# RWKV block kernel: the first pair's place in the projection stream, and the order of a block copy

## The chip, the core and the metric

The kernel runs on one core of a Trainium2 chip. The metric is the time of one execution on the device in microseconds (us), as the median of several runs: 2704.45 us for the kernel before (three runs, 2704.22 to 2705.92). A core has a matrix engine (TensorE, PE in the profile), a vector engine (VectorE, DVE), a scalar engine (ScalarE, ACT), GpSimd (POOL) and a sync engine (SP), each working off its own instructions in order, and 16 DMA engines that they share.

## What is computed

One residual block on 512 tokens of width 2048: a projection, two mixers side by side (RWKV-7 and sliding-window attention), merged by sigmoid gates, and a gated feed-forward layer with a short convolution. Cut to what matters here:

```python
h = rms_norm(x, norm1_g)
z = h @ w_in                       # r, k, v, three low-rank parts; q, k, v; two gates
o_rw = rwkv7_mix(token_shift(z_rw), ...)
o_att = swa_attention(q, k, v, ...)
x = x + (sigmoid(z_r) * (o_rw @ w_b1) + sigmoid(z_a) * (o_att @ w_b2)) @ w_out
x = x + conv_ffn(rms_norm(x, norm2_g), w_up, conv_w, conv_b, w_down)

def rwkv7_mix(...):                # per head, a state of 64 x 64, one token after the other
    def step(state, inp):
        r, k, v, w, ka, kb = inp   # ka = -kk, kb = kk * a, with kk the normalised key
        sa = state @ ka
        state = state * w + outer(sa, kb) + outer(v, k)
        return state, state @ r
    # then a group norm per head, a bonus term, and a gate g
```

## The kernel before

**Stages.** The program projects `z` tile by tile, does the attention while it goes on projecting, then the RWKV mixing, then the branch projection, the output projection, and the feed-forward layer. This case is about the RWKV stage, which in the profile lies between about 306 and 1101 us.

**The projection stream.** A column tile of `z` is 128 columns wide. `ztile` makes one of them by 48 matmuls (`project`, line 284 of the kernel): 16 blocks of the contraction, each taken three times, since weights and activations are split into a high half (`whi`, made by ScalarE at line 263) and a low half (`wlo`, made by VectorE at line 264). Weights come in groups of four blocks, 12 matmuls to a group, each by a DMA on SP's queue (line 260). Every stream matmul is put on the list `stream`, so that other work can be placed against its number. Of the 72 tiles 32 are gate tiles: `emit_gate` makes one, takes its tanh on ScalarE (line 383) and stores it to DRAM from ScalarE's queue. Gates depend on nothing in the RWKV stage and can be made at any time before the branch projection; the kernel uses them to fill TensorE.

**The pairs.** The 16 RWKV heads are done two at a time, as eight pairs `p` = 0 to 7. A pair has two parts:

- `early(p)` projects the pair's key, receptance and value (three tiles of the stream) and makes the decays, the norm of the keys and the bonus. The key norms are summed by small products (line 389), turned by TensorE (line 392), written to DRAM and read back broadcast to all partitions (lines 396 and 400, on SP's queue), and multiplied into `kk` by VectorE (line 675).
- `late(p)` scans. VectorE fills `BKK` and `BAR` (lines 691 to 694); `BAR`'s four writes have to wait for the last product of the pair before that reads `BAR`. TensorE makes the products of keys within 8 chunks of 64 tokens (line 711); VectorE masks them; then a triangular inverse is built up in five doubling levels of two groups of matmuls each (`mm3`, lines 760 and 763), between which ScalarE and VectorE combine results (lines 795 to 799 and 825 to 827). From the second level on, the block made so far is turned by TensorE (`turned`) and copied by `kept` (line 783: three copies on ScalarE, one on VectorE) into `BT`, which the level's second group reads. Last come the 8 chunks in sequence: `psG` (line 836), `psU` (841), the `UV` copies on ScalarE and VectorE (843, 844), `psS` (852), the state `SV` (858).

**What is hung in between.** The output of the pair before is finished inside the levels of the next: `normed` scales it to unit variance on VectorE (its sums begin at line 871, its last instruction, at line 880, scales `y`), right after the first level; `final` turns it, applies the gate and stores it after the fourth level. At the second level the state rows are copied into `UV` (line 805).

**The order of the work.** Loop over pairs: `late(p)`, one gate (not for `p` = 0), `early(p + 1)`, two more gates. So pairs 1 to 6 each bring 288 stream matmuls and pair 0 brings 240. The instructions of the pair would by themselves be issued as early as the planner thinks they can run. Instead the first instruction of each group is held: `entries` lists these (the transposes of the values, the ten groups of the levels, the transposes of `final`, the instructions of the chunks), `at` gives each a number of stream matmuls counted from the pair's `base`, and `behind(ins, stream[base + n - 1])` orders it behind that matmul, without a semaphore, since both are on TensorE. `LEVEL` holds the ten groups' numbers, `CHUNK` those of the chunks. Pair 0 has all of its numbers 4 lower (the first one 7). `pin` keeps marked instructions of an engine in program order.

**Behind the pairs.** The last pair's output is finished by `normed` and `final`, held at 317. The RWKV output is then read back from DRAM, split into halves (`rhi`, `rlo`) between the remaining gates, eight calls of `emit_gate` in all, and the attention output after them (`ahi`, `alo`).

Of the kernel before, what the change touches and what calls it, by code (L numbers as in the profile page):

```python
# [14 lines left out]
ALU = mybir.AluOpType  # L15
# [4 lines left out]
P = 128  # L20
# [3 lines left out]
C = 64  # L24
NCH = S // C
# [110 lines left out]
def block_kernel(ctx: ExitStack, tc: tile.TileContext, d: Dims, a: dict, out: bass.AP):  # L136
    nc = tc.nc
    act, dve, pool, pe, sync = nc.scalar, nc.vector, nc.gpsimd, nc.tensor, nc.sync
    NK, NP, NQ, NKV, NF = d.NK, d.NP, d.NQ, d.NKV, d.NF
# [84 lines left out]
    for f in range(NPRE):  # L224
        w, t = a["w_up"][f], {n: up_d[f, n] for n in ("s3", "s1", "P6", "P3")}
# [26 lines left out]
    def behind(ins, before):  # L252
        tc.add_manual_dep(ins.ins, before.ins.name,
                          mybir.DependencyInfo(mybir.DependencyClass.NoSync, mybir.DependencyReason.DATA))
# [41 lines left out]
    if True:  # L296
# [50 lines left out]
        with tc.tile_pool(name="x0_ps", bufs=1, space=PSUM) as ps0:  # L347
            ps = ps0.tile([P, S], F32, name="ps_r")
# [28 lines left out]
        def emit_gate():  # L377
            if not gates:
                return
            i = gates.pop(0)  # L380
            acc = ztile(d.c_zr + i * P)
            g = wp["gate"].tile([P, S], F32, name="gt", tag="gt")
            act.activation(g, acc, AF.Tanh, scale=0.5)
            act.dma_start(gate_d[i * P : (i + 1) * P], g)
# [19 lines left out]
        with ExitStack() as pt:  # L404
# [87 lines left out]
            for g in range(NHK):  # L492
# [7 lines left out]
                for n in range(NT):  # L500
# [37 lines left out]
                    ps = small()  # L538
# [13 lines left out]
        with ExitStack() as pr:  # L552
# [57 lines left out]
            for h, (lo, hi) in enumerate(HV):  # L610
                ol, oh = HV[1 - h]
# [72 lines left out]
            def late(p, st, norm, finish):  # L684
# [23 lines left out]
                for n0 in range(0, NCH, 2):  # L708
                    ps = bulk()
                    for j in range(2):  # L710
                        pe.matmul(ps[:, j * 2 * P : (j + 1) * 2 * P], BKK[:, n0 + j],  # L711
                                  BAR[:, n0 + j].rearrange("p h a c -> p (h a c)"), start=True, stop=True)
                    src = ps.rearrange("p (n q c) -> p n q c", n=2, q=4)
                    m2 = lambda nm: K[nm].unsqueeze(1).unsqueeze(1).to_broadcast([P, 2, 2, C])
                    dve.tensor_tensor(AB[:, n0 : n0 + 2], src[:, :, 0:4:3], m2("strict"), op=ALU.mult)
                    dve.tensor_tensor(W2[:, n0 : n0 + 2, 1:3], src[:, :, 1:3], m2("incl"), op=ALU.mult)
# [62 lines left out]
                def kept(ps):  # L779
                    dst = BT.rearrange("p e (q w) c -> p e q w c", w=2)  # L780
                    for w, (rl, rh) in enumerate(HV):
                        for h, (lo, hi) in enumerate(HV):
                            (dve.tensor_copy if w and h else act.copy)(dst[lo:hi, :, :, w, lo:hi], ps[rl:rh, :, :, lo:hi])

                for m in LEVELS[1:]:
                    last = m == LEVELS[-1]
# [11 lines left out]
                    dve.tensor_tensor(tt, tt, mask, op=ALU.mult)  # L798
                    done = dve.tensor_tensor(IW[:, :, 1], tt, IW[:, :, 0], op=ALU.subtract)
                    if m == LEVELS[1]:  # L800
                        norm(done)
                    if m == LEVELS[2]:
                        for h in range(2):
                            ol, oh = HV[1 - h]
                            behind(dve.tensor_copy(UV[ol:oh, :, h], SV[ol:oh, :, h]), done)
                    if xt is not None:
                        kept(xt)
                    ps = level_sum()
                    mm3(ps, BT, lambda n: IW[:, n], lambda n: IW[:, n, 0])
                    both = wk.tile([P, 2, NCH, HC], F32, name="tt", tag="dd")  # L810
# [56 lines left out]
            def normed(st, done):  # L867
                y = st[2]
                y3 = r3(y)
                st = wk.tile([P, 2, NCH], F32, name="st", tag="st")  # L870
                first = dve.reduce_sum(st[:, 0], y3, axis=AX.X)
                if done:
                    behind(first, done)
                dve.tensor_scalar(st[:, 0], st[:, 0], -1.0 / HD, None, op0=ALU.mult)
                dve.tensor_tensor(y3, y3, st[:, 0].unsqueeze(2).to_broadcast([P, NCH, C]), op=ALU.add)
                sq = wtile("gn")
                act.activation(sq, y, AF.Square)
                dve.reduce_sum(st[:, 1], r3(sq), axis=AX.X)
                rs = rsqrt_small(wk, st[:, 1], 1.0 / HD, GN_EPS, tag="rg")
                dve.tensor_tensor(y3, y3, rs.unsqueeze(2).to_broadcast([P, NCH, C]), op=ALU.mult)  # L880

            def final(p, st):
                ag, bon, y = st
# [17 lines left out]
                dve.tensor_tensor(yc, yc, ps, op=ALU.mult)  # L901
                pool.dma_start(o_rw_d[p], yc)

            entries = []
            ZT = 3 * NK
            LEVEL = [36, 51, 63, 76, 88, 102, 116, 131, 144, 158]
            CHUNK = [171 + 14 * n + 4 * (n > 2) + x for n in range(NCH) for x in (-5, 0, 4)][1:]
            st, lt, held = early(0), None, []
            for p in range(NP):
                entries.clear()  # L910
                base = len(stream)
                lt = late(p, st, lambda done: lt and normed(lt, done), lambda: lt and final(p - 1, lt))
                if p:
                    emit_gate()
                if p + 1 < NP:
                    st = early(p + 1)
                sums_along(up_jobs)()
                for _ in range(GATES_PER_PAIR * NK // 16 - 1):
                    emit_gate()
                at = [31, *LEVEL[:8], 137, *LEVEL[8:], *CHUNK] if p else [24, *(x - 4 for x in LEVEL + CHUNK)]  # L920
                held += [(ins, base + n - 1) for ins, n in zip(entries, at)]
            entries.clear()
            normed(lt, None)
            final(NP - 1, lt)
# [677 lines left out]
```

## Time and profile before

| what | value |
| --- | --- |
| time, median of three runs | 2704.45 us |
| the profiled execution's own time | 2706.29 us |
| its span, first to last instruction | 2704.5 us |
| mean granted TensorE clock | 0.998 |
| TensorE busy, whole span | 2667.4 us |
| VectorE busy | 1961.5 us |
| ScalarE busy | 1336.7 us |
| GpSimd busy | 232.7 us |

In the lists of waits a line reads: who waited, for what, how many us in total, how often, the longest. In the windows a line is a stretch in us from the span's start, its length, then each engine's busy time and (x) its instructions, the granted TensorE clock (1.00 is full speed), the mean busy share of the DMA engines, and GB/s. In the timeline a line is the start, the busy time, the engine, the line of the kernel, the operation, output and inputs, the shapes and the number of instructions merged into the line; in brackets stands how long the engine had been idle and what ended that. `PEld` is the loading of weights into TensorE, `SPq`, `POOLq` and `ACTq` are instructions of these engines' queues. Names are the program's: `acc` is a projection tile, `bulk` any of the pair's products.

### The profile page before, as it was taken

What the parts mean: (1) busy time and instruction counts of PE and PEld (TensorE: products, weight loads), DVE (VectorE), ACT (ScalarE), POOL (GpSimd) and SP (SyncE); (2) the same over time, 40 slices, a digit from 0 to 9 for tenths busy, and PEclk for the clock granted to TensorE, in tenths of its full rate; (3) what the DMA queues carried; (4) which work ended last, traced back from release to release, by engine and by line L of the source; (5) the groups of instructions that cost most, each with busy time, mean ns of one, the idle gap of its engine ahead of it and who ended that gap; (6) DMA issues with size and microseconds to landing.
All of it is one profiled execution on the core that took longest, in us unless ns stands there. A gap on an engine that the chain in (4) does not pass through costs nothing.

```text
span 2704.5 us, 45690 instructions
## 1 busy us (share of the span) xinstructions
PE 2667.4 (99%) x17410; PEld 1863.9 (69%) x17410; DVE 1961.5 (73%) x3380; ACT 1336.7 (49%) x2229; POOL 232.7 (9%) x323
## 2 busy tenths in 40 slices
PE   8999999999999999999999999999999999999999
PEld 4555566666666666555558999999999998555555
DVE  6787758777877774545678888888888888565665
ACT  6455435544544553322566655555555555444453
POOL 0001111111111101011000111111111110000000
PEclk9999999999999999999999999999999999999999
DMA  6566877889887778889785988988898888877775
GB/s 237 152 165 190 209 205 194 227 217 233 213 222 204 191 185 239 244 242 301 253 269 171 270 233 240 256 248 239 232 250 251 242 236 275 304 240 247 258 259 183
DMA packets 228331, 623.78 MB, mean 231 GB/s; under 512 B 24960, under 2 KB 45072, under 8 KB 227088
## 3 DMA queue, kind: packets, MB, share of 16 engines
q1 hardware_dynamic: 159552, 445.23, 49.4%
q0 software_dynamic: 37216, 136.33, 26.2%
q10 hardware_dynamic: 31344, 39.31, 4.2%
q8 instruction: 136, 2.23, 0.3%
q14 instruction: 83, 0.68, 0.1%
HBM read 571.16 MB, written 191.18 MB: 282 GB/s over the span
## 4 chain that ended last, share of the span: by engine, by line
PE 85%; DVE 7%; DMA 3%; issue 2%; ACT 2%; ACTq 0%; POOL 0%; SPq 0%; DVEq 0%; POOLq 0%
PE acc L284 26%; PE X L1227 18%; PE X L1090 10%; PE Y L1090 9%; PE Y L1227 9%; PE Z L1227 4%; DVE wlo L264 1%; PE psG L836 1%; PE psS L852 1%; PE bulk L711 1%; PE bulk L760 1%; PE mi L541 1%; DMA hraw<-h_dn 1%; DMA h_o<-gin 1%; PE psU L841 1%
## 5 line engine op out<-in xcount | busy, mean ns | idle before, releaser
L1081 DVE TENSOR_TENSOR wlo<-raw,whi 128x1024 bf16<-128x1024 f32 x210 | 256.5, 1224 | 192.0 <-ACT whi L1080 190.7
L284 PE MATMUL acc<-xhi,whi 128*128 128x512 f32 x1152 | 347.1, 425 | 10.4 <-ACT whi L263 10.4
L1080 ACT ACTIVATE whi<-raw 128x1024 fp32r<-128x1024 f32 x210 | 221.8, 1058 | 274.2 <-PE X L1090 124.5
L263 ACT ACTIVATE whi<-raw 128x512 fp32r<-128x512 f32 x352 | 218.6, 627 | 254.0 <-PE acc L284 149.0
L264 DVE TENSOR_TENSOR wlo<-raw,whi 128x512 bf16<-128x512 f32 x352 | 239.5, 687 | 136.9 <-ACT whi L263 104.8
L284 PE MATMUL acc<-xlo,whi 128*128 128x512 bf16 x1152 | 316.2, 383 | 0.7 <-DVE xlo L314 0.4
L284 PE MATMUL acc<-xlo,wlo 128*128 128x512 bf16 x1072 | 293.5, 380 | 0.0
L1227 PEld LDWEIGHTS <-wlo 128*128 128x128 bf16 x2464 | 237.6, 96 | 39.6 <-DVE wlo L1209 0.7
L284 PEld LDWEIGHTS acc<-xhi,whi 128*128 128x128 f32 x1152 | 211.7, 189 | 58.5 <-ACT whi L263 11.8
L1227 PEld LDWEIGHTS <-whi 128*128 128x128 bf16 x2464 | 228.0, 98 | 33.1 <-issue 0.2
L284 PEld LDWEIGHTS <-wlo 128*128 128x128 bf16 x1408 | 137.8, 100 | 150.0 <-issue 8.8
L284 PEld LDWEIGHTS <-whi 128*128 128x128 bf16 x1408 | 125.8, 101 | 151.6 <-issue 49.6
L1209 DVE TENSOR_TENSOR wlo<-raw,whi 128x1024 bf16<-128x1024 f32 x184 | 224.0, 1218 | 5.9 <-ACT whi L1207 5.8
L1207 ACT ACTIVATE whi<-a 128x1024 fp32r<-128x1024 f32 x124 | 130.7, 1054 | 191.6 <-DVE a L1202 188.9
L1207 ACT ACTIVATE whi<-raw 128x1024 fp32r<-128x1024 f32 x184 | 193.0, 1050 | 42.0 <-issue 21.8
L1209 DVE TENSOR_TENSOR wlo<-a,whi 128x1024 bf16<-128x1024 f32 x124 | 151.9, 1225 | 71.6 <-ACT whi L1207 71.6
L1227 PE MATMUL X<-b,whi 128*128 128x256 f32 (+1 forms) x1472 | 195.2, 280 | 0.2 <-DVE x L1105 0.2
L1227 PE MATMUL Y<-t,whi 128*128 128x256 f32 (+1 forms) x1408 | 186.2, 280 | 0.0
L1227 PE MATMUL X<-t,whi 128*128 128x256 bf16 (+1 forms) x1408 | 185.4, 280 | 0.0
L1280 DVE SCALAR_TENSOR_TENSOR c<-u,par,c 128x512 f32<-128x512 f32 x176 | 131.5, 748 | 41.8 <-ACT c L1271 41.7
L1090 PEld LDWEIGHTS <-hhi 128*128 128x128 bf16 x840 | 81.5, 97 | 104.1 <-issue 0.3
L1090 PEld LDWEIGHTS <-hlo 128*128 128x128 bf16 x840 | 72.8, 97 | 107.4 <-issue 27.9
(390 smaller groups left out, 4591.6 us busy)
## 6 DMA issues: line engine op xcount, KB each, us to landing
raw<-in_w_up_dram SPq DMA_DIRECT2D x170, 512.0 KB
raw<-in_w_z_dram SPq DMA_DIRECT2D x288, 256.0 KB
s_dn<-in_w_dn_dram POOLq DMA_DIRECT2D x88, 512.0 KB, 7.2
raw<-s_dn SPq DMA_DIRECT2D x88, 512.0 KB
raw<-in_w_up_dram POOLq DMA_DIRECT2D x80, 512.0 KB, 8.6
raw<-in_w_dn_dram SPq DMA_DIRECT2D x66, 512.0 KB
s_dn<-in_w_dn_dram SPq DMA_DIRECT2D x44, 512.0 KB
s_dn<-s_dn SPq DMA_DIRECT2D x44, 512.0 KB
```

What stands on the lines that cost most here:

```text
L263: act.activation(hi, raw, AF.Copy)
L264: dve.tensor_tensor(lo, raw, hi.bitcast(F32), op=ALU.subtract)
L284: stream.append(pe.matmul(acc, l, r, start=k0 + j == 0, stop=k0 + n == nk and j == len(ops) - 1))
L541: pe.matmul(ps, vhl[:, n - 1 + kb, g].rearrange("p e c -> p (e c)"), phl[i][:, kb].rearrange("p h c -> p (h c)"), start=kb == kbs[0] and i ...
L711: pe.matmul(ps[:, j * 2 * P : (j + 1) * 2 * P], BKK[:, n0 + j], BAR[:, n0 + j].rearrange("p h a c -> p (h a c)"), start=True, stop=True)
L1080: act.activation(whi, wr, AF.Copy)
L1081: dve.tensor_tensor(wlo, wr, whi.bitcast(F32), op=ALU.subtract)
L1090: pe.matmul(dst, l, r, start=fst and j == order[0], stop=lst and j == order[2], skip_group_check=True)
L1207: pin(act.activation(hi, t, AF.Copy))
L1209: return lambda: pin(dve.tensor_tensor(lo, t, hi.bitcast(F32), op=ALU.subtract))
L1227: pin(pe.matmul(ps, l, r, start=start and k == 0 and i == way[0], stop=k == KH - 1 and i == way[2], skip_group_check=True))
L1280: pin(dve.scalar_tensor_tensor(t, u[:, i, j + 1 : j + 1 + S], cw[:, j + 1, ci : ci + 1], t, op0=ALU.mult, op1=ALU.add))
```

## The change

Four things are changed.

1. `emit_gate()` behind `late(p)` is called for pair 0 as well. Pair 0 then has 288 stream matmuls, and since there are 32 gates in all, the last of the calls behind the pairs finds none left.
2. Pair 0's numbers are no longer 4 lower than the others' but 8 higher (`lag`), pair 1's are 4 higher, the other pairs' unchanged. Four of the ten level numbers are one higher for all pairs: 63, 76, 88 and 158 become 64, 77, 89 and 159.
3. The first product of pair 0 (line 711 of the kernel before) is held behind the twelfth stream matmul from the pair's base; no pair's first product was held before.
4. At the second level `kept` is called ahead of the copies of the state rows, and both these copies and the last scaling of `normed` are ordered behind `kept`'s copy on VectorE. At the other levels the call moves ahead only in the text. These are orders on one engine, without a semaphore.

```diff
@@ -708,8 +708,10 @@
                 for n0 in range(0, NCH, 2):
                     ps = bulk()
                     for j in range(2):
-                        pe.matmul(ps[:, j * 2 * P : (j + 1) * 2 * P], BKK[:, n0 + j],
-                                  BAR[:, n0 + j].rearrange("p h a c -> p (h a c)"), start=True, stop=True)
+                        ins = pe.matmul(ps[:, j * 2 * P : (j + 1) * 2 * P], BKK[:, n0 + j],
+                                        BAR[:, n0 + j].rearrange("p h a c -> p (h a c)"), start=True, stop=True)
+                        if n0 + j == 0:
+                            grams.append(ins)
                     src = ps.rearrange("p (n q c) -> p n q c", n=2, q=4)
                     m2 = lambda nm: K[nm].unsqueeze(1).unsqueeze(1).to_broadcast([P, 2, 2, C])
                     dve.tensor_tensor(AB[:, n0 : n0 + 2], src[:, :, 0:4:3], m2("strict"), op=ALU.mult)
@@ -780,7 +782,8 @@
                     dst = BT.rearrange("p e (q w) c -> p e q w c", w=2)
                     for w, (rl, rh) in enumerate(HV):
                         for h, (lo, hi) in enumerate(HV):
-                            (dve.tensor_copy if w and h else act.copy)(dst[lo:hi, :, :, w, lo:hi], ps[rl:rh, :, :, lo:hi])
+                            ins = (dve.tensor_copy if w and h else act.copy)(dst[lo:hi, :, :, w, lo:hi], ps[rl:rh, :, :, lo:hi])
+                    return ins
 
                 for m in LEVELS[1:]:
                     last = m == LEVELS[-1]
@@ -798,13 +801,14 @@
                     dve.tensor_tensor(tt, tt, mask, op=ALU.mult)
                     done = dve.tensor_tensor(IW[:, :, 1], tt, IW[:, :, 0], op=ALU.subtract)
                     if m == LEVELS[1]:
-                        norm(done)
+                        scaled_y = norm(done)
+                    part = kept(xt) if xt is not None else None
                     if m == LEVELS[2]:
+                        if scaled_y:
+                            behind(scaled_y, part)
                         for h in range(2):
                             ol, oh = HV[1 - h]
-                            behind(dve.tensor_copy(UV[ol:oh, :, h], SV[ol:oh, :, h]), done)
-                    if xt is not None:
-                        kept(xt)
+                            behind(dve.tensor_copy(UV[ol:oh, :, h], SV[ol:oh, :, h]), part)
                     ps = level_sum()
                     mm3(ps, BT, lambda n: IW[:, n], lambda n: IW[:, n, 0])
                     both = wk.tile([P, 2, NCH, HC], F32, name="tt", tag="dd")
@@ -877,7 +881,7 @@
                 act.activation(sq, y, AF.Square)
                 dve.reduce_sum(st[:, 1], r3(sq), axis=AX.X)
                 rs = rsqrt_small(wk, st[:, 1], 1.0 / HD, GN_EPS, tag="rg")
-                dve.tensor_tensor(y3, y3, rs.unsqueeze(2).to_broadcast([P, NCH, C]), op=ALU.mult)
+                return dve.tensor_tensor(y3, y3, rs.unsqueeze(2).to_broadcast([P, NCH, C]), op=ALU.mult)
 
             def final(p, st):
                 ag, bon, y = st
@@ -901,24 +905,25 @@
                 dve.tensor_tensor(yc, yc, ps, op=ALU.mult)
                 pool.dma_start(o_rw_d[p], yc)
 
-            entries = []
-            ZT = 3 * NK
-            LEVEL = [36, 51, 63, 76, 88, 102, 116, 131, 144, 158]
+            entries, grams = [], []
+            LEVEL = [36, 51, 64, 77, 89, 102, 116, 131, 144, 159]
             CHUNK = [171 + 14 * n + 4 * (n > 2) + x for n in range(NCH) for x in (-5, 0, 4)][1:]
             st, lt, held = early(0), None, []
             for p in range(NP):
                 entries.clear()
                 base = len(stream)
                 lt = late(p, st, lambda done: lt and normed(lt, done), lambda: lt and final(p - 1, lt))
-                if p:
-                    emit_gate()
+                emit_gate()
                 if p + 1 < NP:
                     st = early(p + 1)
                 sums_along(up_jobs)()
                 for _ in range(GATES_PER_PAIR * NK // 16 - 1):
                     emit_gate()
-                at = [31, *LEVEL[:8], 137, *LEVEL[8:], *CHUNK] if p else [24, *(x - 4 for x in LEVEL + CHUNK)]
-                held += [(ins, base + n - 1) for ins, n in zip(entries, at)]
+                at = [31, *LEVEL[:8], *([137] if p else []), *LEVEL[8:], *CHUNK]
+                lag = max(0, 8 - 4 * p)
+                held += [(ins, base + n + lag - 1) for ins, n in zip(entries, at)]
+                if p == 0:
+                    held.append((grams[0], base + 11))
             entries.clear()
             normed(lt, None)
             final(NP - 1, lt)
```

## The prediction

> **What bounds the kernel now.** I read the page's first part and its chain first, then the waits of TensorE over the RWKV stage, then windows pair by pair, and then the order of instructions around each wait that this gave.
>
> ```profile
> span 2704.5 us, 45690 instructions
> PE 2667.4 (99%) x17410; PEld 1863.9 (69%) x17410; DVE 1961.5 (73%) x3380; ACT 1336.7 (49%) x2229; POOL 232.7 (9%) x323
> PE 85%; DVE 7%; DMA 3%; issue 2%; ACT 2%; ACTq 0%; POOL 0%; SPq 0%; DVEq 0%; POOLq 0%
> ```
>
> TensorE is busy for 99% of the span and is 85% of the chain: whatever it idles, or does at a lower clock, is paid in full. The change adds and removes no matmul, so its worth is idle time of TensorE. In the RWKV stage that is little and well named (waited for: us in total, times, longest):
>
> ```profile
> PE psS L852 <- DVE UV L844: 4.9, 1, 4.9
> PE bulk L711 <- DVE BAR L693: 2.4, 1, 2.4
> PE bulk L760 <- DVE BT L783: 2.0, 6, 0.3
> PE bulk L760 <- DVE XIW L799: 1.5, 3, 0.6
> PE bulk L760 <- DVE XIW L827: 1.1, 2, 0.8
> PE bulk L711 <- DVE bon L681: 0.4, 1, 0.4
> ```
>
> Together 12.3 us. The windows say in which pair they fall: the first three rows run from the start of pair 0, 1 and 2 to the start of the next, then come the wait ahead of pair 0's first product, the wait of 4.9 us, and the stretch behind it.
>
> ```profile
> 306.27:404.94 98.67, 90.10 (x612) 58.98 (x612) 68.08 (x155) 42.28 (x92) 10.96 (x16) 0.97 0.78 202
> 404.94:493.34 88.40, 86.06 (x603) 56.42 (x603) 69.61 (x172) 42.14 (x93) 9.96 (x16) 1.00 0.81 206
> 493.34:586.20 92.86, 92.34 (x636) 61.11 (x635) 71.10 (x172) 45.08 (x98) 12.08 (x18) 1.00 0.86 224
> 306.27:308.63 2.36, 0.00 (x1) 0.04 (x1) 2.31 (x5) 0.59 (x2) 0.00 (x0) 1.00 1.03 335
> 374.90:380.08 5.18, 0.27 (x2) 0.00 (x1) 2.83 (x6) 0.63 (x1) 0.00 (x0) 0.85 1.06 303
> 380.08:385.15 5.07, 5.07 (x17) 3.05 (x17) 3.90 (x7) 0.00 (x0) 0.91 (x2) 0.50 0.48 120
> ```
>
> Idle time is length less TensorE's busy time: 8.57 us in pair 0, 2.34 in pair 1, 0.52 in pair 2, which stands for pairs 2 to 7. Pair 0 loses more than it idles: for 5.07 us behind the long wait the granted clock is 0.50, so half of that, 2.5 us, is lost to the clock. The prices sit in the first two pairs, which the change lays out anew.
>
> **The change part by part.** One matmul of the projection stream costs 0.223 us (120.72 / 541, the chain of waits behind the last pair); a gate's 48 cost 10.7.
>
> ```profile
> 1054.65 120.72 PE acc L284 x541
> ```
>
> Two conversions of VectorE at pair 0's start, and the tanh of a gate in the list of groups:
>
> ```profile
> 307.79 0.68 DVE L693 SCALAR_TENSOR_TENSOR BAR<-kk,Et 64x512 f32<-64x512 f32 x1
> 308.51 1.29 DVE L264 TENSOR_TENSOR wlo<-raw,whi 128x512 bf16<-128x512 f32 x2
> ```
> ```profile
> L383 ACT ACTIVATE gt<-acc 128x512 f32<-128x512 f32 x32 | 19.1, 597 | 65.9 <-PE acc L284 65.9
> ```
>
> *Gate ahead of pair 0, first product held back.* The gate's 48 matmuls now come where the key projection of early(1) came, and pair 0's first product waits for 12 of them: 12 x 0.223 = 2.7 us of work where TensorE stood idle for 2.36. L693, its input, ends at 308.5 and should be ready. The danger is VectorE, busy for 2.31 of those 2.36 us: the low halves of the gate's weights must be made before or beside it, one at 0.65 (half of the 1.29 row). With two of them pushed ahead of L693 the gain is 1.1; with none 2.36. I take 2.1, nearer the upper end, since the two conversions at 308.51 come behind L693 already and the stream ran on without a wait for them. The wait for bon (0.4) and pair 0's part of the XIW wait (0.6) come from the same crowded VectorE; the distances from first product to first groups hardly change (24 to 27 and 47 to 47 stream matmuls), so of this 1.0 I take 0.3 (0 to 1.0). With the gate go its four weight loads on SP, ahead of early(1)'s loads, the weight sum on SP and POOL that its loads count off, and a tanh and a store on ACT: the same instructions, one gate earlier, on queues with room (POOL 10.96 and ACT 42.28 busy of 98.67 in pair 0); I charge nothing, and at most the 0.6 of the tanh (L383) if ACT were full. Behind the held product wait only pair 0's own products and transposes.
>
> *Pair 0 with 288 stream matmuls in place of 240.* Its long wait is a chain:
>
> ```profile
> 362.27 0.27 PE L392 MATMUL bulk<-ident,rq 128*8 128x128 f32 x1 [0.15 <-DVE rq L207]
> 362.89 0.29 SPq L396 DMA_DIRECT2D rsd<-rsT  x1
> 368.99 1.11 SPq L400 DMA_DIRECT2D rsb<-rsd  x2
> 373.68 0.38 PE L841 MATMUL psU<-GY,BX 128*128 128x128 f32 x2
> 377.16 0.69 DVE L675 TENSOR_TENSOR kk<-kk,rsb 128x512 f32<-128x512 f32 x1 [5.04 <-DMA rsb<-rsd]
> 379.80 0.23 DVE L844 COPY UV<-psU 64x64 f32<-64x64 f32 x1
> ...
> 547.90 0.27 PE L392 MATMUL bulk<-ident,rq 128*8 128x128 f32 x1
> 552.15 1.12 SPq L400 DMA_DIRECT2D rsb<-rsd  x2
> 558.86 0.68 DVE L675 TENSOR_TENSOR kk<-kk,rsb 128x512 f32<-128x512 f32 x1
> 560.39 0.23 DVE L844 COPY UV<-psU 64x64 f32<-64x64 f32 x1 [0.26 <-ACT UV L843]
> ```
>
> The key norms of the next pair go through DRAM and back: from L392 to L675 14.9 us in pair 0, 11.0 in pair 2, where VectorE did not wait. In pair 0 VectorE stands at L675 for 5.04 us with the UV copy of a chunk behind it, whose product was ready at 373.7 + 0.4; TensorE runs dry at psS. Only pair 0 is packed so that early(1) must be through 86 stream matmuls (240 less 154) after its last level; the new layout gives 121 (288 less 167), and 130 are there in pairs 2 to 7, none of which has this wait. I take all of it: 4.9 + 2.5 = 7.4; if the trip is late again, none.
>
> [...]
>
> *Groups later in pair 1.* Pair 0's chunks ran 33 matmuls into pair 1 (273 against 240) and now end at 285 of 288. Pair 1 starts its levels with a free VectorE and 4 matmuls, 0.9 us, of extra room. Its 2.34 should fall towards the 0.52 of pair 2; I take 1.9 (1.0 to 2.34). The seam itself is not short: the first product of pair 1 came 3.5 us behind pair 0's last psG without a wait,
>
> ```profile
> 401.45 0.56 PE L836 MATMUL psG<-SV,BAR 128*128 128x64 f32 x4
> 404.94 3.69 PE L711 MATMUL bulk<-BAR,BKK 128*128 128x256 f32 x16
> ```
>
> and will have 13 stream matmuls (2.9 us), psU and psS between (0.38 for psU by its row, as much taken for psS), about 3.7 us.
>
> *Block copy first, six pairs.* At the second level of pair 2 VectorE goes:
>
> ```profile
> 517.49 0.42 DVE L799 TENSOR_TENSOR XIW<-tt,XIW 128x256 f16<-128x256 f32 x1
> 517.83 0.68 DVE L880 TENSOR_TENSOR yc<-yc,rg 128x512 f32<-128x512 f32 x1
> 518.53 0.86 DVE L805 COPY UV<-SV 64x512 f32<-64x512 f32 x2
> 519.41 0.43 DVE L783 COPY BT<-bulk 64x512 f16<-64x512 f16 x1
> 520.96 0.42 DVE L826 SCALAR_TENSOR_TENSOR tt<-bulk,XIW 128x256 f32<-128x256 f32 x1 [0.39 <-ACT XIW L825]
> ```
>
> With L783 right behind L799 the copy ends near 518.3 and not 519.84, 1.5 us earlier, and the group is held one matmul later. The 0.33 of each pair should go: 1.8 of 2.0 (1.0 to 2.0). Scaling and state copies, 1.54 us, then run in the room ahead of L826; what waits on them is far off (the output's transposes stand at 137, the chunks at 171). The other positions that move by one cost nothing: stream matmuls fill the place.
>
> *One gate less at the end.* The last group, at 317, has 163 stream matmuls behind it before the branch projection in place of 211.
>
> ```profile
> 1092.31 1.28 DVE L217 TENSOR_TENSOR rlo<-rin,rhi 128x512 bf16<-128x512 f32 x2
> 1102.34 4.91 DVE L217 TENSOR_TENSOR alo<-ain,ahi 128x512 bf16<-128x512 f32 x8 [3.05 <-ACT ahi L216]
> 1107.76 1.89 DVE L264 TENSOR_TENSOR wlo<-raw,whi 128x512 bf16<-128x512 f32 x3
> ```
>
> The last two halves of the RWKV output were made at 1092, a gate ahead of the attention halves at 1102; now they come beside these and can push the weight halves behind them by 1.28. TensorE did not wait there; I charge 0.3 (0 to 1.3).
>
> **Sum.** 2.1 + 0.3 + 7.4 + 1.9 + 1.8 - 0.3 = 13.2 us. The profiled execution took 2706.29 us, 1.84 above the median of 2704.45, so 2693.1 there and 2691.3 as a median. With all upper ends 15.1 (2689.4); with all lower ends but the long wait gone 9.2 (2695.3).
>
> **The rivals.** *The long wait comes back.* The trip's length may be a matter of DMA load and not of layout: over the long wait the DMA engines' share was 1.06, and L675 precedes the UV copy in pair 2 as well, which is only 12.5 us behind L392. A trip of 14.9 us would again stop VectorE. For it: the two legs took 6.1 and 8.2 us in pair 0. Against: no other pair waits. Price: the 7.4 stays, 13.2 - 7.4 = 5.8, so 2698.7. [...]
>
> *Given back later.* Behind the stage the transfers of the weight sums and of the stored factors have their own pace; if one of them is what really holds TensorE at the next stage, the gain is lost there. Against it: the chain from 1054 on is TensorE without a break for 120 us, and transfers are issued as loads are used, so they move along. Price: most of the 13, 2702 to 2705.
>
> *Slower: scaling and state copies push the next level.* They now stand ahead of L826 in six pairs. L826 may start until about 520.9 (now 520.96, less the 0.33, plus one matmul); with L783 ending at 518.3, 1.54 of copies and one weight half (0.65) it starts near 520.5. Should more of VectorE's queue move ahead of it, all beyond 0.4 us is paid six times. To end slower by 5.4 it takes (13.2 + 5.4) / 6 = 3.1 us per pair, five weight halves: 2710 or more. For it: in pair 1 the same chain made TensorE wait, 1.1 us at L827. Against: VectorE idles 0.39 just there.
>
> **How the numbers follow.** Forecast 0.70; the long wait back 0.14; given back 0.10; slower 0.06. Measurement of this kernel can tell about 0.2%, 5.4 us, from no change: faster means below 2699.0. The rival at 2698.7 lies on that edge; I count 0.09 of its 0.14 as faster. Faster 0.79, same 0.15, slower 0.06. The range of 2689 to 2699 holds the forecast's own 2689.4 to 2695.3 and that part of the first rival.
>
> **What would show it.** In the changed profile: no wait of psS for UV above 0.5 us and no clock of 0.50 within the stage; L711's first wait under 0.5; L760's six waits for BT gone; pair 1's idle time under 1 us; branch projection entered without a wait. A wait of DVE at L675 for rsb with psS behind it makes the first rival right; waits at L760 for XIW L827 in every pair the last; all waits gone and the same time, the second.

## The result and the profile after

The changed kernel takes 2716.19 us (median; 2703.11 to 2718.24) beside 2704.53 us (2697.18 to 2706.68) of the kernel before in the same measurement: a ratio of 1.0033, with a 95% interval of 1.0021 to 1.0046. It is slower by about 12 us, where 13 us less was forecast. Its profiled execution took 2716.8 us.

The first lines of its page:

```profile
span 2715.0 us, 45687 instructions
PE 2669.1 (98%) x17410; PEld 1867.8 (69%) x17410; DVE 1964.5 (72%) x3380; ACT 1337.8 (49%) x2229; POOL 233.9 (9%) x323
```

The matmuls are the same 17410 and TensorE's busy time grew by 1.7 us only, so the other 9 us are idle time. One window finds the place: from the first key-norm product (L392, ahead of pair 0) to the first transposes behind the output projection. In the kernel before:

```profile
286.84:1415.05 1128.21, 1113.65 (x6727) 693.10 (x6728) 772.47 (x1661) 499.76 (x994) 121.83 (x183) 1.00 0.82 226
```

and in the changed one:

```profile
286.52:1425.75 1139.23, 1115.55 (x6727) 697.00 (x6728) 774.41 (x1661) 500.41 (x994) 122.61 (x182) 0.99 0.81 224
```

The same 6727 matmuls take 11.0 us longer: idle time grows from 14.56 to 23.68 us, and busy time by 1.9 us, which I put down to the clock (its rows follow). The whole loss lies in this stretch. TensorE's waits there, in the changed kernel (psG, psU, UV and psS now stand at lines 840, 845, 848 and 856, the products of the levels at 762 and 765, the block copy at 785):

```profile
PE psS L856 <- DVE UV L848: 15.5, 5, 6.1
PE bulk L392 <- DVE rq L207: 3.0, 7, 0.5
PE acc L284 <- DVE rlo L217: 1.4, 2, 1.2
PE bulk L711 <- DVE bon L681: 1.0, 1, 1.0
PE bulk L762 <- DVE XIW L802: 0.3, 1, 0.3
PE bulk L762 <- DVE XIW L831: 0.3, 1, 0.3
```

Most of the forecast gains are there. The six waits for BT are gone, the waits for XIW fell from 2.6 to 0.6 us, and at pair 0's start 1.0 us for bon is left of 2.8. But the wait of psS for UV, which was to vanish, came five times, 15.5 us in place of 4.9. The windows of the first three pairs, and those where the clock was granted at half:

```profile
308.47:406.28 97.81, 89.52 (x614) 59.14 (x613) 66.50 (x153) 41.28 (x90) 10.99 (x16) 0.97 0.82 204
406.28:503.36 97.08, 93.80 (x636) 61.85 (x636) 71.92 (x174) 45.41 (x98) 11.88 (x17) 0.98 0.81 210
503.36:597.99 94.63, 92.47 (x637) 61.30 (x636) 71.41 (x173) 45.13 (x98) 11.76 (x17) 1.00 0.84 217
378.41:385.24 6.83, 3.30 (x10) 2.81 (x11) 5.40 (x11) 0.63 (x1) 0.81 (x1) 0.50 0.50 129
477.40:480.81 3.41, 3.18 (x10) 1.99 (x11) 2.83 (x7) 0.00 (x0) 0.00 (x0) 0.50 0.69 208
668.54:675.37 6.83, 6.17 (x19) 3.77 (x20) 5.01 (x10) 0.27 (x1) 1.42 (x3) 0.50 0.98 218
```

Before, pair 0 idled 8.57 us, pair 1 2.34 and pair 2 0.52. Now pair 0 idles 8.29 us, pair 1 3.28 and pair 2 2.16. Here is one of the new waits from beginning to end, in the part of pair 2 where early(3) runs (rows of the changed kernel's timeline):

```profile
553.50 0.50 SPq L242 DMA_DIRECT2D s_dn<-in_w_dn_dram  x1
...
557.82 0.27 PE L392 MATMUL bulk<-ident,rq 128*8 128x128 f32 x1 [0.43 <-DVE rq L207]
...
558.97 0.29 SPq L396 DMA_DIRECT2D rsd<-rsT  x1
...
559.32 0.50 SPq L242 DMA_DIRECT2D s_dn<-in_w_dn_dram  x1
...
563.80 1.12 SPq L400 DMA_DIRECT2D rsb<-rsd  x2
...
569.65 0.38 PE L845 MATMUL psU<-GY,BX 128*128 128x128 f32 x2
...
570.90 0.69 DVE L675 TENSOR_TENSOR kk<-kk,rsb 128x512 f32<-128x512 f32 x1 [2.03 <-DMA rsb<-rsd]
...
572.23 0.23 DVE L848 COPY UV<-psU 64x64 f32<-64x64 f32 x1
...
572.51 0.66 PE L856 MATMUL psS<-UV,W 128*128 128x64 f32 x4 [1.61 <-DVE UV L848]
```

The trip of the key norms through DRAM, L392 to L675, takes 13.1 us; in the kernel before it took 11.0 in the same pair. VectorE stands at L675 for 2.03 us, the copy of UV waits behind it in the same queue though its product is ready at 570.0, and TensorE runs dry. Two rows are new beside the norms' write at 558.97: weight sums at 553.50 (5.5 us ahead) and at 559.32 (0.35 us behind). The same queue in the kernel before:

```profile
542.03 0.50 SPq L242 DMA_DIRECT2D s_dn<-in_w_dn_dram  x1
...
549.16 0.29 SPq L396 DMA_DIRECT2D rsd<-rsT  x1
...
554.03 0.50 SPq L242 DMA_DIRECT2D P_u<-P_u  x1
...
555.21 0.51 SPq L242 DMA_DIRECT2D s_dn<-in_w_dn_dram  x1
```

There the sums stood 7.1 us ahead and 4.9 and 6.1 us behind the write: the second and third came only after the norms' read (552.15).

**What a weight sum is, and why it moved.** `sums_along` adds two quarters of a weight of the output projection (`s_o`) or of the feed-forward layer (`s_dn`), which are used in later stages: a copy within DRAM on SP's queue, then an adding DMA on GpSimd's. `load_w` calls it by a count of weight loads: after every third load, and ten more times 12 loads apart:

```python
extra = range(6 * NK + 5, 6 * NK + 5 + 12 * (HELD // 3), 12)
...
wp["n"] += 1
...
elif wp["n"] % wp["step"] == 0 or wp["n"] in extra:
    sums_along()()
```

A pair of 288 stream matmuls has 24 loads, a whole number of both cycles, so every pair gets its sums at the same places. Pair 0 had 20 loads and now has 24: **the moved gate's four loads shift the sums of all later pairs by four loads.** The extra ones came at a pair's 1st and 13th load, and now come at its 9th and 21st. The trip of the key norms falls at about the 22nd load. With only ten of them, an extra sum stands ahead of the norms' write in pairs 0 to 4 alone (5.5 to 7.9 us ahead), and these are the five pairs that wait; in pairs 5 and 6, without one, the trips took 11.4 and 11.0 us.

**The theories.** A: the sums' new places lengthen the norms' trip; VectorE stands at L675 with the UV copy behind it. A2 (formed on the way): what hurts is an extra sum about 5.5 us ahead of the norms' write together with a regular one right behind it. B: the new layout itself makes the trip or the chunk late, wherever the sums are. C: the room that a mended wait gives back is lost to another wait. D: the seven new waits at L392 come of the last level's group being held at 159 in place of 158.

### The profile page after: what moved, and what is told of

Its sections match the earlier page's. It is cut to its first block, busy times and chain, and to the rows that moved or that the text cites. A ratio compares the mean times of both kernels' runs of the same rounds, so it can differ in the third digit from the quotient of the medians.

```text
span 2715.0 us, 45687 instructions
## 1 busy us (share of the span) xinstructions
PE 2669.1 (98%) x17410; PEld 1867.8 (69%) x17410; DVE 1964.5 (72%) x3380; ACT 1337.8 (49%) x2229; POOL 233.9 (9%) x323
## 4 chain that ended last, share of the span: by engine, by line
PE 89%; DVE 4%; DMA 3%; issue 2%; ACT 1%; POOL 0%; SPq 0%; DVEq 0%; ACTq 0%; POOLq 0%
PE acc L284 29%; PE X L1232 18%; PE X L1095 11%; PE Y L1095 9%; PE Y L1232 9%; PE Z L1232 4%; PE psS L856 1%; DMA rsb<-rsd 1%; PE psG L840 1%; PE bulk L762 1%; PE bulk L711 1%; PE mi L541 1%; DMA xi<-in_x_dram 1%; DVE wlo L264 1%; DMA rsd<-rsT 1%
## 5 line engine op out<-in xcount | busy, mean ns | idle before, releaser
L284 PE MATMUL acc<-xhi,whi 128*128 128x512 f32 x1152 | 348.1, 426 | 10.4 <-ACT whi L263 10.1
L284 PE MATMUL acc<-xlo,whi 128*128 128x512 bf16 x1152 | 318.1, 383 | 0.7 <-DVE xlo L314 0.4
L284 PE MATMUL acc<-xlo,wlo 128*128 128x512 bf16 x1072 | 293.6, 381 | 0.0
L284 PEld LDWEIGHTS acc<-xhi,whi 128*128 128x128 f32 x1152 | 213.3, 190 | 60.5 <-ACT whi L263 11.6
L284 PEld LDWEIGHTS <-wlo 128*128 128x128 bf16 x1408 | 138.1, 99 | 152.2 <-issue 11.2
L284 PEld LDWEIGHTS <-whi 128*128 128x128 bf16 x1408 | 126.3, 101 | 152.3 <-issue 50.5
```

The costliest lines, as they stand in the source:

```text
L284: stream.append(pe.matmul(acc, l, r, start=k0 + j == 0, stop=k0 + n == nk and j == len(ops) - 1))
```

## The experiments

**Sums shifted back in the changed kernel.** The count is raised by 2 ahead of pair 0's gate, which puts the extra sums at a pair's 7th and 19th load and the regular ones where pairs 1 to 7 of the kernel before had them.

```diff
+                if p == 0:
+                    wp["n"] += 2
                 emit_gate()
```

> The changed kernel, with the count of weight loads by which the weight sums are issued (every third load) advanced by 2 ahead of pair 0's gate, so that in every pair the sums come at the loads at which they came in pairs 1 to 7 of the kernel before. Theory A (the gate's four loads shifted the sums by one load against the key norms' trip through DRAM, and a sum's 512 KB now travels with it): the sum on SP is issued 4 to 5 us behind the norms' write and not 0.3 to 2.4, the write's leg (to the issue of the read back) is 2.4 to 3.5 us in most pairs, psS waits for UV less than 3 us in all (15.5 in the changed kernel), the clock is 1.00 through the stage, 2692 to 2699 us. Theory B (the new positions themselves, groups later and block copy first, bring the wait; the sums have no part): 10 to 16 us of psS waiting for UV, 2710 to 2718 us.

Measured: 2700.96 us (2695.22 to 2705.48), ratio 0.9988 (0.9979 to 0.9997). Nothing of the layout was undone, and 15 us were gone. The median lies 2 us above A's range; in the profiled execution (2695.22, the fastest of its twelve) three shorter waits of psS remain:

```profile
PE psS L856 <- DVE UV L848: 3.6, 3, 1.6
```

Two of them, in pairs 3 and 4, follow trips of 13.1 and 12.2 us that had a single sum near, 7.4 us ahead of the write. A trip can then be late with one sum too.

**Sums shifted in the kernel before.** The count is lowered by 2 at the end of pair 0. The regular sum then comes 0.3 us behind the norms' write in pairs 2 to 5 and 0.4 in pair 6, as in the changed kernel, but the extra ones do not come ahead of it.

```diff
                 held += [(ins, base + n - 1) for ins, n in zip(entries, at)]
+                if p == 0:
+                    wp["n"] -= 2
```

> The kernel before, with nothing changed but the count of weight loads set back by 2 at the end of pair 0, so that in pairs 1 to 7 the sums come at the loads at which they come in the changed kernel. Theory A: the wait of psS for UV appears in two to five of the trips that follow pair 0's, 6 to 14 us in all beside the 4.9 of pair 0, with half clock behind the longer ones: 2711 to 2722 us. Theory B: as the kernel before, 4.9 us of such waits and 2702 to 2707 us.

Measured: 2704.43 us (2701.3 to 2709.96), ratio 0.9998 (0.999 to 1.0007). A missed: the regular sum right behind the write harms nothing by itself; the trips of pairs 2 to 6 stayed at 11.0 us, and only pair 0 waits, for 1.7 us. That led to A2.

```profile
PE psS L852 <- DVE UV L844: 1.7, 1, 1.7
```

**An intermediate shift of the changed kernel.** As in the first experiment, by 1 in place of 2. In pairs 1 to 4 the extra sum then comes 7.4 us ahead of the norms' write and the regular one 5.5 us ahead, and none right behind it. In pair 2:

```profile
541.40 0.55 SPq L242 DMA_DIRECT2D s_dn<-in_w_dn_dram  x1
...
543.34 0.50 SPq L242 DMA_DIRECT2D s_dn<-in_w_dn_dram  x1
...
548.81 0.29 SPq L396 DMA_DIRECT2D rsd<-rsT  x1
```

> The changed kernel, with the count advanced by 1 ahead of pair 0's gate: the third of the three possible phases, every sum one load (about 3.6 us) earlier against the trip than in the changed kernel, so that SP's half of a sum comes 3 to 4 us ahead of the norms' write and GpSimd's half lands on the trip. Theory A: the trip still has company, write leg 4 to 6 us, psS waits 3 to 12 us in all, 2698 to 2712 us. Theory B: as the changed kernel, 2710 to 2718 us with 10 to 16 us of waits.

Measured: 2710.76 us (2703.61 to 2714.81), ratio 1.0016 (1.0007 to 1.0026), between the two kernels and within A's range:

```profile
PE psS L856 <- DVE UV L848: 10.4, 6, 3.0
```

Six waits, 10.4 us in the profiled execution (2704.72, one of the faster ones). The five largest are those of pair 0 and of pairs 1 to 4, whose trips took 12.1 to 14.4 us with both sums ahead of the write; with the regular sum alone at 5.5 us ahead, in pairs 5 and 6, they took 11.0 and 11.7. So the two places that A2 names are too narrow: two sums near the trip cost a good part also when both stand ahead of the write.

**VectorE's scaling of the keys held behind a UV copy.** The sums stay where the change put them. L675 alone is ordered behind the UV copy of the fourth chunk of the pair that is scanned, so VectorE no longer stands ahead of the copy that TensorE needs.

```diff
+            uvs = []
...
-                pin(dve.tensor_tensor(kk, kk, rb, op=ALU.mult))
+                ins = pin(dve.tensor_tensor(kk, kk, rb, op=ALU.mult))
+                if uvs:
+                    behind(ins, uvs[3])
...
+                uvs.clear()
...
-                    dve.tensor_copy(UV[C:P, n, 1], ps[C:P, 1])
+                    uvs.append(dve.tensor_copy(UV[C:P, n, 1], ps[C:P, 1]))
```

> The changed kernel, with VectorE's product of the keys with their norms (line 675) ordered behind the UV copy of the fourth chunk, about 17 us behind the turning of the norms, in place of ahead of the third chunk's copy. The sums stay where the change put them. Theory A and theory B both say that the trip is as long as before (11 to 16 us) but stops nothing: psS waits under 2 us in all, clock 1.00, 2692 to 2699 us. A rival C (the transfers on the DMA engines are what is late, and whatever needs them next waits instead: the weight halves or the next pair's first products): the waits turn up at L284 or L711, and the time stays above 2704 us.

Measured: 2696.64 us (2693.63 to 2699.12), ratio 0.9967 (0.9955 to 0.9979). One instruction moved, and 19.6 us of the changed kernel's time are gone. The waits above 0.3 us in the stage are then

```profile
PE bulk L392 <- DVE rq L207: 3.0, 7, 0.5
PE acc L284 <- DVE rlo L217: 1.5, 2, 1.3
```

No wait for UV, no half clock in the stage, and nothing has turned up in its place: C fell. The same part of pair 2, by its timeline (L677 is the scaling, L853 the UV copy):

```profile
546.03 0.27 PE L392 MATMUL bulk<-ident,rq 128*8 128x128 f32 x1 [0.42 <-DVE rq L207]
...
553.90 1.12 SPq L400 DMA_DIRECT2D rsb<-rsd  x2
...
558.53 0.23 DVE L853 COPY UV<-psU 64x64 f32<-64x64 f32 x1 [0.26 <-ACT UV L852]
...
564.29 0.23 DVE L853 COPY UV<-psU 64x64 f32<-64x64 f32 x1
...
564.54 0.69 DVE L677 TENSOR_TENSOR kk<-kk,rsb 128x512 f32<-128x512 f32 x1
```

The scaling now comes 18.5 us behind L392 and waits for nothing, and early(3) is none the worse for it: there was room all along.

**The ten extra sums moved alone.** The layout stays changed and the regular sums stay where they are; the extra ones come three loads later.

```diff
-    extra = range(6 * NK + 5, 6 * NK + 5 + 12 * (HELD // 3), 12)
+    extra = range(6 * NK + 8, 6 * NK + 8 + 12 * (HELD // 3), 12)
```

> The changed kernel, with the list of extra weight sums (ten loads, twelve apart, at which a sum is issued beside every third load) moved by three loads, so that in each pair an extra sum falls on loads 0 and 12 and no more on 9 and 21; the sums at every third load stay where the change put them. Theory A2 (the trip of the key norms is late where an extra and a regular sum stand within some 6 us of each other around it; one sum alone is harmless): the extra sum at 5.5 us ahead of the norms' write is gone in trips 2 to 5, the trip falls to 11.0 us there without a wait, psS waits 0 to 4 us in all (pair 0 may keep some), 2695 to 2702 us. Theory B2 (the layout makes the trip late by itself, the regular sum at 0.3 us being enough there): 10 to 16 us of psS waits, 2710 to 2718 us.

Measured: 2699.49 us (2695.07 to 2702.51), ratio 0.9981 (0.9973 to 0.999), within A2's range. Trips of pairs 1 to 6 are back at 10.5 to 11.8 us, and of psS's waits pair 0's 2.5 us and 0.4 are left:

```profile
PE psS L856 <- DVE UV L848: 2.9, 2, 2.5
```

**The changed kernel's sum places in the old layout.** The kernel before, with its count lowered by 8 at the end of pair 0, which brings the regular sums of pairs 1 to 6 and the extra ones of pairs 1 to 4 where the changed kernel has them by their trips; one extra sum comes ahead of pair 5's trip in place of pair 0's. No other part of the change is made.

```diff
+                if p == 0:
+                    wp["n"] -= 8
```

> The kernel before, with nothing changed but the count of loads set back by 8 at the end of pair 0, so that in pairs 1 to 5 both the regular and the extra sums come at the very loads of a pair at which they come in the changed kernel (extras on loads 9 and 21). Theory A2: an extra sum appears 5 to 6 us ahead of the norms' write beside the regular one at 0.3, trips of 12 to 15 us, psS waits in most of the trips 2 to 5, 5 to 12 us in all beside pair 0's, 2709 to 2720 us. Theory B2: trips of 11.0 us in pairs 1 to 7, as with the regular sums shifted alone, 2702 to 2707 us.

Measured: 2717.1 us (2708.62 to 2720.6), ratio 1.0045 (1.0032 to 1.0058). The old layout with the new sum places is as slow as the changed kernel. Its largest wait in the stage (those for BT are as before, 2.0 us), and one of the late trips:

```profile
PE psS L852 <- DVE UV L844: 12.0, 5, 4.6
```

```profile
543.11 0.50 SPq L242 DMA_DIRECT2D s_dn<-in_w_dn_dram  x1
...
547.04 0.27 PE L392 MATMUL bulk<-ident,rq 128*8 128x128 f32 x1
...
548.30 0.29 SPq L396 DMA_DIRECT2D rsd<-rsT  x1
...
548.64 0.50 SPq L242 DMA_DIRECT2D s_dn<-in_w_dn_dram  x1
...
554.66 1.12 SPq L400 DMA_DIRECT2D rsb<-rsd  x2
...
561.32 0.69 DVE L675 TENSOR_TENSOR kk<-kk,rsb 128x512 f32<-128x512 f32 x1 [3.23 <-DMA rsb<-rsd]
```

Sums stand 5.2 us ahead of the norms' write and 0.3 behind it, and the trip takes 14.3 us where it took 11.0: the changed kernel's picture, without its layout. B falls. Pair 5 of this run has both sums too and no wait (11.0 us), so the two sums make a late trip likely and not certain.

**The hold in the kernel before.** The same edit at L675.

> The kernel before with only VectorE's line 675 ordered behind the fourth chunk's UV copy, as in the run that held it in the changed kernel. Both theories: pair 0's wait of 4.9 us and its half clock go, nothing else moves: 7.4 us by the sum of the prediction, so 2696 to 2699 us. Then the changed kernel held in the same way (2696.6) is worth 0 to 3 us more or less than the old layout, and what was forecast for the rest of the change (6 us) was given back inside it. If it is at 2702 or more, the hold costs something that the first run of it hid.

Measured: 2700.51 us (2698.4 to 2706.43), ratio 0.999 (0.9981 to 0.9998), a little above what was expected: at the median 3 to 4 us are won by it, not the 7.4 that the prediction read from the profiled execution with its long wait. The times of the kernel before spread over 9 us (2697.18 to 2706.68), so its wait need not be 4.9 us in each execution. In the profiled one two sums stood near pair 0's trip, an extra one 2.3 us ahead of the norms' write and a regular one 1.0 us behind it; they belong to pair 1's first two loads, which are issued that early. In the two runs of the old layout with a shifted count only one stands there, 2.3 us ahead, and pair 0's wait is 1.7 and 1.2 us. So the old long wait too looks like a matter of sums; no run moved that sum alone.

**Last level's group back at 158, with the hold, in the changed kernel.**

```diff
-            LEVEL = [36, 51, 64, 77, 89, 102, 116, 131, 144, 159]
+            LEVEL = [36, 51, 64, 77, 89, 102, 116, 131, 144, 158]
```

> The changed kernel with line 675 held, and the last level's second group back at 158 from 159. The changed kernel has a new wait of 0.38 to 0.50 us at line 392 in seven pairs, behind the chain of 13 small instructions of VectorE that starts when the last level's products are through. Theory D (that one matmul of delay at the last level is what makes the chain late): the waits at L392 fall below 0.25 each, 1.5 us in all are won, 2694 to 2696 us against 2696.6. Theory E (the chain is late because the block copy or other work of VectorE moved): the waits stay at 0.4 and the time at 2696 to 2697.

Measured: 2695.67 us (2692.64 to 2695.91), ratio 0.9967 (0.9954 to 0.998). The waits at L392 fall from seven to two:

```profile
PE bulk L392 <- DVE rq L207: 0.7, 2, 0.5
```

D is right for the waits. The time's 1 us against the hold alone is within the spread of either.

**The block copy behind the state copies again, with the hold, in the changed kernel.** This undoes the fourth part of the change alone.

```diff
-                    part = kept(xt) if xt is not None else None
                     if m == LEVELS[2]:
-                        if scaled_y:
-                            behind(scaled_y, part)
                         for h in range(2):
                             ol, oh = HV[1 - h]
-                            behind(dve.tensor_copy(UV[ol:oh, :, h], SV[ol:oh, :, h]), part)
+                            behind(dve.tensor_copy(UV[ol:oh, :, h], SV[ol:oh, :, h]), done)
+                    if xt is not None:
+                        kept(xt)
```

> The changed kernel with the hold (kk's scaling behind the fourth UV copy) and with the fourth part of the change alone undone: at the second level the state copies and the scaling of y go ahead of the turned block's copy again. The prediction priced this part at 1.8 us (1.0 to 2.0), six waits of TensorE for BT of about 0.33 each. If that price is right: six waits for BT at the third level's product come back, about 2 us together, and the time is 2698 to 2699 beside 2696.6 with the hold alone. Rival: TensorE's first product of the second group is then late for another input as well (XIW or the next level's group), because the copies only changed places: fewer or no BT waits and a time within 0.7 us of 2696.6.

Measured: 2702.52 us (2699.17 to 2706.98), ratio 0.9995 (0.9986 to 1.0004), more than was expected. The waits for BT are back, with one in pair 0 as well:

```profile
PE bulk L766 <- DVE BT L789: 2.6, 7, 0.4
...
PE bulk L715 <- DVE bon L685: 1.1, 1, 1.1
...
PE bulk L715 <- DVE BAR L697: 0.6, 1, 0.6
```

The rival (waits that only change places) fell. Between the two profiled executions (2700.76 with this edit, 2696.75 with the hold alone) lie 4.0 us: 2.6 are the waits for BT, and 1.7 are waits at pair 0's start that this edit does not touch and that come and go between executions (0.98 us for bon in the changed kernel, none with the hold). The medians lie 5.9 us apart; what is beyond these waits is not accounted for.

**All three mends together** in the changed kernel: the hold, 158, and the extra sums three loads later.

```diff
-    extra = range(6 * NK + 5, 6 * NK + 5 + 12 * (HELD // 3), 12)
+    extra = range(6 * NK + 8, 6 * NK + 8 + 12 * (HELD // 3), 12)
...
-            LEVEL = [36, 51, 64, 77, 89, 102, 116, 131, 144, 159]
+            LEVEL = [36, 51, 64, 77, 89, 102, 116, 131, 144, 158]
```

> The changed kernel with all three mends: the hold, the last level's number back from 159 to 158, and the ten extra weight sums moved by three loads. Theory: with the hold, VectorE's stand at the scaling of kk costs TensorE nothing, so moving the sums as well wins nothing more: 2695 to 2697, as with the hold and 158 alone (2695.7). Rival: the late sums also cost elsewhere in the stage, or their move keeps the norms' trip short enough that early work behind kk is ahead in the next pair: 2692 to 2694. No wait of psS for UV in either case; waits at L392 under 0.5 in at most two pairs.

Measured: 2694.3 us (2693.08 to 2697.51), ratio 0.9971 (0.996 to 0.9983). It falls between the two ranges, and its interval overlaps those of the hold alone and of the hold with 158: once VectorE no longer stands ahead of the copy, where the sums lie cannot be told from the time. These three are the fastest versions measured, each about 0.3% below the kernel before.

## Why the prediction was wrong

**The failed step** is the largest term of the sum, 7.4 us for pair 0's long wait: "Only pair 0 is packed so that early(1) must be through 86 stream matmuls" and, with 121 in the new layout, "I take all of it". Two things were wrong in it.

- *The measure of room.* The stream matmuls left behind the last level say when early(p + 1) must end. The wait hangs on another distance, from L392 to the next UV copy that stands behind L675 on VectorE, and that the new layout did not change. The rows give it: a trip less the wait that it caused is 10.0 us in pair 0 before (14.9 less 4.9) and 9.9 to 10.0 in the changed kernel (16.1 less 6.1) and in the five runs that move sums; it is 10.8 to 10.9 in pair 1 and 11.5 in pairs 2 to 4, in both layouts. So pair 0 does have less room than the others, but not for want of stream matmuls: 35 more of them left it as it was. VectorE has three more instructions between L675 and that UV copy in pair 0, by either kernel's timeline, and one in pair 2. Since pair 0's room lies below the 11.0 us of a usual trip, it waits in every one of the seven profiles without the hold. Pair 0's psU stood ready 11.4 + 0.4 us behind L392 before (362.27 and 373.68), and 11.2 + 0.4 after, by the changed kernel's timeline:

```profile
362.92 0.27 PE L392 MATMUL bulk<-ident,rq 128*8 128x128 f32 x1 [0.40 <-DVE rq L207]
...
364.29 0.39 SPq L396 DMA_DIRECT2D rsd<-rsT  x1
...
372.57 1.11 SPq L400 DMA_DIRECT2D rsb<-rsd  x2
...
374.10 0.39 PE L845 MATMUL psU<-GY,BX 128*128 128x128 f32 x2
...
379.01 0.69 DVE L675 TENSOR_TENSOR kk<-kk,rsb 128x512 f32<-128x512 f32 x1 [6.24 <-DMA rsb<-rsd]
...
381.94 1.11 PE L856 MATMUL psS<-UV,W 128*128 128x64 f32 x4 [6.14 <-DVE UV L848]
```

 The trip took 16.1 us, longer still than the 14.9 before. The prediction had this distance in hand ("L675 precedes the UV copy in pair 2 as well, which is only 12.5 us behind L392") and used it for the rival alone. Pairs 1 to 6 did not wait because L675 began there 10.5 to 11.2 us behind L392, within their room of 10.8 to 11.5, and not because of 130 matmuls. Since VectorE hardly stood at L675 in them (0.18 us at most), the norms themselves may have arrived earlier still.
- *The cover of the moved work.* "The weight sum on SP and POOL that its loads count off" was seen, and priced at nothing as the "same instructions, one gate earlier". It is not one sum: the count runs on, and the shift by four loads moved the sums of every later pair. The busy time of POOL and SP says nothing here; what matters is which transfers stand next to a trip that has 10.0 to 11.5 us of room. The forecast had no row of SP's queue for it.

**The first rival** ("the long wait comes back") was the right mechanism: a trip whose length is a matter of DMA traffic, with L675 ahead of the UV copy. It was given 0.14 and the price of one pair, 7.4 us. In the profiled execution five pairs waited, 15.5 us, and three stretches ran at half clock. The two experiments that move sums alone show the mechanism from both sides: out of the way in the new layout (2699.5), in the way in the old (2717.1).

**The other terms.**

- Block copy first, 1.8 us: right. The 2.0 us of waits are gone, and 2.6 come back when this part alone is undone.
- Pair 1, 1.9 us: the waits for XIW fell from 2.6 to 0.6 us over all pairs, about what pair 1 was charged; but pair 1's idle time rose from 2.34 to 3.28 us, 2.49 of which is the new wait.
- Start of pair 0, 2.1 + 0.3: the wait for BAR is gone, that for bon is 1.0 in place of 0.4. 1.4 to 1.8 of 2.4 came, and differs from execution to execution.
- The tail, 0.3 charged with 1.3 as its bound: 1.4 measured (L284 for rlo), the bound and not the chosen value. VectorE's two halves now do come late.
- "The other positions that move by one cost nothing": wrong by the seven waits at L392, 3.0 us, that the last level's 159 brought.

Taken together, with the hold in both, so that the long wait is out of both: from the first L392 to the first transposes behind the output projection the old layout took 1121.4 us (287.32 to 1408.68), the changed one 1117.0 (287.35 to 1404.39), and 1115.8 with 158 (288.72 to 1404.54). That is 4.3 and 5.5 us won where the terms beside the long wait add up to 5.8. The medians, 2700.51 and 2696.64, say 3.9. So the change does most of what its other steps were priced at, and the waits that the hold removes cost 19.6 us on top. Moving the ten extra sums alone won 16.7 of these (2716.19 to 2699.49).

What is left open: by which way the sums delay the trip. From the write's issue to the read's it took 4.8 to 10.5 us in pairs 0 to 4 of the changed kernel, against 2.4 to 6.1 before, and no run separated waiting in SP's queue from sharing the DMA engines or the memory. Nor is it settled what sets pair 0's own trip, which ran from 11.2 to 16.1 us in the profiled executions without the hold, or why the first experiment's pairs 3 and 4 were late with one sum near.

## What to carry to other kernels

When work is issued by a count (every third load, every twelfth), a moved block shifts everything that is counted behind it: work out where each item lands in every later round, and look at what it lands beside. When an in-order engine may have to stand for a round trip, measure the distance from the trip's start to the next urgent instruction behind the stand, and compare it with the trip's longest time seen, not its usual one; ordering the waiting instruction behind the urgent one cost nothing here and won 19.6 us.

## What the runs showed of the hardware

- Half clock followed idle times of TensorE of 4.91 us in the kernel before (375.17) and of 6.14, 2.49 and 3.69 us in the changed one (375.80, 475.14, 665.51); the stretches last 3.41 or 6.83 us. Across the 2.36 us at the old pair 0's start (306.27) and the 1.62 us in the changed kernel's pair 2 (570.89) the granted clock stayed at 1.00. In the intermediate shift the longest wait of psS is 3.0 us, and the mean granted clock of the execution is 0.999, beside 0.996 in the changed kernel. Whether the length of an idle time decides alone was not shown.
- The price of a half-clock stretch was less than half its length here. From the kernel before to the changed one, TensorE's busy time in the stretch from L392 to the transposes grew by 1.9 us (1113.65 to 1115.55), although 17.1 us of half clock stand there in place of 6.8 (6.83 + 3.41 + 6.83). Part of a stretch falls on idle time: TensorE was busy for 12.65 us of the 17.07.
- A trip of the key norms through DRAM and back took from 11.0 to 16.1 us within the changed kernel's profiled execution, with the same instructions each time; moving other transfers alone brought it to 10.5 to 12.5.
